# Operand sums of the feed-forward Strassen products moved from VectorE to ScalarE and accumulating DMAs, and three plain gate/up pairs a layer in place of four

## The chip, the cores and the metric

The kernel runs on one core of one Trainium2 chip. The time is the device time of one execution in microseconds (us), the median of several runs. The engines are TensorE (PE), VectorE (DVE), ScalarE (ACT), GpSimd (POOL) and SyncE (SP). Each engine takes its instructions in the order in which they stand in its own queue, and an instruction that waits holds up all that stand behind it.

## The reference

A two-layer decoder trunk on 512 positions of width 1024, all float32. Layer 0 mixes positions by dilated window attention, layer 1 by causal pooling; each is followed by a SwiGLU feed-forward part, with RMSNorm ahead of every part. The change is in the feed-forward part alone:

```
def rmsnorm(x, g):
    y = x * lax.rsqrt(jnp.mean(x * x, axis=-1, keepdims=True) + RMS_EPS)
    return y * g

def swiglu_ffn(h, w_gate_up, w_down):        # D_FF = 2816 = 22 blocks of 128
    gu = h @ w_gate_up
    gate, up = gu[..., :D_FF], gu[..., D_FF:]
    return (jax.nn.silu(gate) * up) @ w_down

x = x + swiglu_ffn(rmsnorm(x, ffn_norm[i]), w_ffn_gate_up[i], w_ffn_down[i])
```

## The kernel before

Positions lie along the free dimension (512 columns), channels along the 128 partitions: x is eight tiles X[0] to X[7] of 128x512. Every float32 operand of a large product is split into two parts, `hi` (a rounded copy, by ACT) and `lo` (the rest, by DVE; `split`, L93 and L94, or `split_neg`, L97 and L98, for the negated value), and every product is three matmuls: hi by hi, hi by lo, lo by hi.

The feed-forward part (`ffn`) makes 22 gate/up pairs j = 0 to 21 and then the down products. A **plain pair** is two products of 8 k-steps by 3 matmuls of 512 columns, 48 matmuls (`Product.add`, L314 to L317). A **Strassen pair** (`chained`, with `mult`, L446 to L448) cuts gate and up, the channels and the positions into halves and needs seven products of 4 k-steps by 3 matmuls of 256 columns, 84 matmuls. The first `NPLAIN` = 4 pairs of a layer are plain, since the operands of the Strassen pairs must first be made out of the normalised x. In layer 0 the first part of the layer is pairs 0 to 5, and its down products follow; in layer 1 the first part is pairs 0 and 1, and their down products (8 products of 2 k-steps, 48 matmuls of 512) stand behind the plain pairs (`PARTS`).

The plain pairs do not wait for the normalisation: `lead` holds two and five eighths of their products ahead of it, on x times its weight, and each result is multiplied by the row of 1/rms (`row`, made on ACT at L415) when it is read out (L1029, L1035).

The operands of the Strassen pairs are made by `prepare(k)` for half pair k = 0 to 3, that is, for channel blocks k and k + 4. `normed` writes both normalised blocks to a buffer `h` (two L563 on DVE, 128x512 each). Its four quarters of 256 columns are h[0,0], h[0,1] (first block, left and right positions) and h[1,0], h[1,1]. DVE then makes the four sums "1" = h[0,1] - h[0,0], "2" = "1" - h[1,1], "3" = h[1,1] - h[1,0] and "4" = "2" + h[1,0] (negated), at L567, L568 and L570, into a second buffer. All operands are split: "11" and "21" (the left quarters), the sums, and "22" (negated). Both buffers are `Temp`, taken from two loose slots (`slot`), and are given back at the end of `prepare`. Each plain pair calls `prepare(j)` once.

Weights come by DMAs on SP's queue into four `raw` buffers, are split into five `w` buffers, and a Strassen pair's sums of weights are made by an accumulating DMA on POOL's queue (L161) and two additions on DVE (L177, L178). `pump`, called behind each product, issues loads and splits when buffers are free. The order on each engine is set by a scheduler when the program is built; it may put instructions of later calls ahead of earlier ones where their data allow it.

Of the kernel before, what the change touches and what calls it, by code (L numbers as in the profile page):

```python
# [10 lines left out]
AF = mybir.ActivationFunctionType  # L11
OP = mybir.AluOpType
# [4 lines left out]
S = 512  # L17
# [19 lines left out]
NF = 4  # L37
H2 = S // 2
K2 = KC // 2
NPLAIN = 4  # L40
WARM = 6
NSOLO = 3
PARTS = {0: ((0, 6, False), (6, 14, True), (14, 22, True)), 1: ((0, 2, False), (2, 10, True), (10, 18, True), (18, 22, False))}
# [21 lines left out]
def trunk(ctx: ExitStack, tc: tile.TileContext, xT, xN, norms, w_first, w_qk, w_qkp, w_v0, w_v0p, w_v12, w_out, w_pair, w_down, w_dblock, w_pin, w_pgrp,  # L65
          consts, ident_in, invcnt_in, outT, outR):
    nc = tc.nc
# [24 lines left out]
    def split(hi, lo, v):  # L92
        nc.scalar.activation(hi, v, AF.Copy)  # L93
        nc.vector.tensor_tensor(lo, v, hi.bitcast(F32), op=OP.subtract)  # L94

    def split_neg(hi, lo, v):
        nc.scalar.activation(hi, v, AF.Copy, scale=-1.0)  # L97
        nc.vector.scalar_tensor_tensor(lo, v, -1.0, hi.bitcast(F32), op0=OP.mult, op1=OP.subtract)  # L98
# [251 lines left out]
    held = {}  # L350

    def give(key):
        del taken[held.pop(key)]
# [202 lines left out]
        def done(self):  # L556
            del taken[self.i]

    def normed(layer, k, row, h, t, chained=False):

        for i in range(2):
            c = k + i * K2
            nc.vector.scalar_tensor_tensor(h.t[:, i * S:(i + 1) * S], X[c], nrm[:, layer, c:c + 1], row,  # L563
                                           op0=OP.mult, op1=OP.mult)
        hq = h.t.rearrange("p (a b c) -> p a b c", a=2, b=2)
        tq = t.t.rearrange("p (a b c) -> p a b c", a=2, b=2)
        nc.vector.tensor_sub(tq[:, :, 0], hq[:, :, 1], hq[:, 0])  # L567
        nc.vector.tensor_sub(t.t[:, H2:S], t.t[:, :H2], h.t[:, 3 * H2:])  # L568
        if chained:
            nc.vector.scalar_tensor_tensor(t.t[:, 3 * H2:], t.t[:, H2:S], -1.0, h.t[:, S:3 * H2], op0=OP.mult, op1=OP.subtract)  # L570
        else:
            nc.vector.tensor_add(t.t[:, 3 * H2:], t.t[:, H2:S], h.t[:, S:3 * H2])
        return h, t

    def halves_of(hi, lo):
        return [tuple(v[:, a * H2:(a + 1) * H2] for v in (hi, lo)) for a in range(2)]
# [8 lines left out]
    with tc.tile_pool(name="opool", bufs=1) as opool:  # L585
        early = opool.tile([P, HEADS, S], F32R, tag="o", name="early")
        with tc.tile_pool(name="apool", bufs=1) as apool:
            const = apool.tile([P, 5 * P], F32, name="const")
            d0, d12, swap = const[:, :2 * G], (const[:, 2 * G:2 * G + P], const[:, 2 * G + P:3 * G]), const[:, 3 * G:3 * G + P]
            rows = {}  # L590
# [250 lines left out]
            H, T, o = {}, {}, []  # L841

            def prepare(k):

                h, t = normed(0, k, rows["row"], Held("raw"), Held("raw"))
# [88 lines left out]
            for c in range(2):  # L934
                p = product(0)
# [69 lines left out]
    with tc.tile_pool(name="fpool", bufs=2) as fpool:  # L1005
# [3 lines left out]
        def ftile(name, n=S):  # L1009
            return fpool.tile([P, PAD + S], F32, tag="f", name=name, bufs=6)[:, :n]  # L1010
# [8 lines left out]
        def ffn(layer, nxt, lead, row):  # L1019

            op = nxt - 1
# [4 lines left out]
            def plain_pair(j, up):  # L1026
                pg = gu()
                gt = ftile("gt")
                nc.vector.tensor_mul(gt, pg, row)  # L1029
                prepare(j)  # L1030
                pu = gu()
                if j == NPLAIN - 1:
                    for k in range(KC):
                        give((op, k))
                nc.vector.tensor_mul(up, pu, row)  # L1035
                nc.scalar.activation(gt, gt, AF.Silu)
                nc.vector.tensor_mul(up, up, gt)

            T = {}

            def prepare(k):


                h, t = normed(op, k, row, Temp(), Temp(), True)
                hq, b22 = h.t.rearrange("p (a b c) -> p a b c", a=2, b=2), h.t[:, 3 * H2:]
# [3 lines left out]
                for i, names in enumerate((("1", "2"), ("3", "4"))):  # L1049
                    held["t", k, 1 + i], b = slot("tt", apart=True)  # L1050
                    split(b[:, 0], b[:, 1], t.t[:, i * S:(i + 1) * S])
                    for a, name in enumerate(names):
                        T[name, k] = tuple(b[:, e, a * H2:(a + 1) * H2] for e in range(2))
# [3 lines left out]
                split_neg(*n, b22)  # L1057
                T["22", k] = n
                h.done()
                t.done()  # L1060

            B, U, late = {}, {}, deque()

# [27 lines left out]
            def operands_left(i, v):  # L1091
# [5 lines left out]
            def later(f, *a):  # L1097
                return lambda: f(*a)

            def waiting():  # L1100
                hooks = {}
# [54 lines left out]
            j = 0  # L1156
# [280 lines left out]
```

## Time and profile before

| | |
|---|---|
| median of 3 runs | 1197.54 us (1196.87 to 1197.91) |
| the profiled execution | 1197.8 us |
| its span | 1196.0 us |
| granted TensorE clock | 0.998 |
| TensorE busy | 1184.6 us (99%) |
| VectorE busy | 997.2 us (83%) |
| ScalarE busy | 680.7 us (57%) |
| GpSimd busy | 147.0 us (12%) |

The span is the stretch from the first to the last instruction; 1.8 us of the profiled execution lie around it. Matmuls overlap each other in the records, so what one costs is the distance from its start to the next one's start, not its own duration. The feed-forward part of layer 0 begins with the row of 1/rms on ACT at 485.91 us of the span, that of layer 1 at 873.45 us.

### The profile page before, as it was taken

Reading aid. Unit: us, or ns where it says so; the run is one execution under the profiler, and the core shown is the slowest. Engines: PE = TensorE matmul, PEld = TensorE weight load, DVE = VectorE, ACT = ScalarE, POOL = GpSimd, SP = SyncE. Lnnn points to the kernel's source line nnn. Section 1 sums busy time; section 2 is a strip of 40 time slices with the busy share of each in tenths; the row PEclk is TensorE's granted clock in tenths of the full one; section 3 lists DMA queues with packets and bytes.
Section 4 is the critical chain, followed back from the end, with each engine's and each line's share of the span. In section 5 each row is a group of like instructions: output and inputs, shape, how many; then the busy total and the mean of one; then the engine's idle time right before and its main releaser. Section 6 shows DMA issues by size and latency. Waiting matters only on the chain.

```text
span 1196.0 us, 24858 instructions
## 1 busy us (share of the span) xinstructions
PE 1184.6 (99%) x9936; PEld 1118.9 (94%) x9936; DVE 997.2 (83%) x1730; ACT 680.7 (57%) x1214; POOL 147.0 (12%) x137
## 2 busy tenths in 40 slices
PE   9999999999999999999999999999999999999997
PEld 7889999999999988898999999998789999999996
DVE  6978898889788856895899889998989998898875
ACT  6445564555456643562677567763455776676553
POOL 1111211111111000101111111100310111111100
PEclk9999999999999999999999999999999999999999
DMA  8346656665766533336677777753153777777732
GB/s 277 124 103 163 156 154 161 170 159 150 189 149 163 163 133 122 88 115 158 160 197 188 194 201 199 186 171 124 53 122 93 191 196 198 196 191 199 189 86 72
DMA packets 73365, 188.42 MB, mean 158 GB/s; under 512 B 7312, under 2 KB 9504, under 8 KB 73248
## 3 DMA queue, kind: packets, MB, share of 16 engines
q1 hardware_dynamic: 50400, 141.98, 36.1%
q0 software_dynamic: 22704, 44.58, 23.1%
q8 instruction: 78, 1.28, 0.4%
q14 instruction: 39, 0.32, 0.1%
q10 hardware_dynamic: 144, 0.26, 0.1%
HBM read 184.70 MB, written 2.10 MB: 156 GB/s over the span
## 4 chain that ended last, share of the span: by engine, by line
PE 87%; DVE 6%; issue 3%; ACT 1%; DMA 1%; POOL 0%; SPq 0%; POOLq 0%; DVEq 0%; ACTq 0%
PE ps L446 19%; PE ps L447 18%; PE ps L448 18%; PE ps L314 7%; PE ps L315 7%; PE ps L317 7%; PE ps L617 2%; PE ps L619 2%; PE ps L618 2%; DVE w L94 2%; PE ps L829 1%; PE ps L701 1%; DVE s L1225 1%; ACT w L93 1%; PE ps L721 1%
## 5 line engine op out<-in xcount | busy, mean ns | idle before, releaser
L93 ACT ACTIVATE w<-raw 128x1024 fp32r<-128x1024 f32 (+1 forms) x299 | 313.5, 1056 | 213.7 <-PE ps L448 69.1
L94 DVE TENSOR_TENSOR w<-raw,w 128x1024 fp32r<-128x1024 f32 (+1 forms) x299 | 361.5, 1214 | 58.9 <-ACT w L93 55.5
L446 PE MATMUL ps<-far,w 128*128 128x256 f32 x916 | 251.9, 275 | 0.1
L447 PE MATMUL ps<-far,w 128*128 128x256 f32 x916 | 251.8, 275 | 0.0
L448 PE MATMUL ps<-far,w 128*128 128x256 f32 x916 | 251.8, 275 | 0.0
L446 PE MATMUL ps<-near,w 128*128 128x256 f32 x632 | 178.4, 282 | 0.4 <-ACT first L528 0.4
L447 PE MATMUL ps<-near,w 128*128 128x256 f32 x632 | 174.8, 277 | 0.0
L448 PE MATMUL ps<-near,w 128*128 128x256 f32 x632 | 174.8, 277 | 0.0
L446 PEld LDWEIGHTS ps<-far,w 128*128 128x128 f32 x916 | 171.8, 188 | 0.6 <-ACT first L528 0.5
L447 PEld LDWEIGHTS ps<-far,w 128*128 128x128 f32 x916 | 171.9, 188 | 0.1
L448 PEld LDWEIGHTS ps<-far,w 128*128 128x128 f32 x916 | 171.9, 188 | 0.0
L446 PEld LDWEIGHTS ps<-near,w 128*128 128x128 f32 x632 | 118.9, 188 | 1.3 <-ACT first L528 0.9
L447 PEld LDWEIGHTS ps<-near,w 128*128 128x128 f32 x632 | 118.8, 188 | 0.0
L448 PEld LDWEIGHTS ps<-near,w 128*128 128x128 f32 x632 | 118.8, 188 | 0.0
L315 PE MATMUL ps<-near,w 128*128 128x512 f32 (+1 forms) x284 | 106.6, 375 | 0.6 <-DVE near L379 0.6
L314 PE MATMUL ps<-near,w 128*128 128x512 f32 (+1 forms) x284 | 106.9, 377 | 0.0
L317 PE MATMUL ps<-near,w 128*128 128x512 f32 (+1 forms) x284 | 106.1, 374 | 0.0
L161 POOL DMA_DIRECT2D raw<-w_pair x36 | 43.6, 1212 | 359.7 <-DMA raw<-w_pair 174.8
L315 PEld LDWEIGHTS ps<-near,w 128*128 128x128 f32 x284 | 53.4, 188 | 11.0 <-DVE near L379 1.8
L317 PEld LDWEIGHTS ps<-near,w 128*128 128x128 f32 x284 | 53.3, 188 | 9.5
L314 PEld LDWEIGHTS ps<-near,w 128*128 128x128 f32 x284 | 53.3, 188 | 9.4
L93 ACT ACTIVATE half<-rawhalf 128x512 fp32r<-128x512 f32 x81 | 51.0, 631 | 14.7 <-PE ps L448 12.5
(315 smaller groups left out, 2749.7 us busy)
## 6 DMA issues: line engine op xcount, KB each, us to landing
raw<-w_pair SPq DMA_DIRECT2D x80, 512.0 KB, 4.3
raw<-w_qkp SPq DMA_DIRECT2D x36, 512.0 KB, 4.1
raw<-w_pair POOLq DMA_DIRECT2D x36, 512.0 KB, 7.4
raw<-w_dblock SPq DMA_DIRECT2D x32, 512.0 KB, 4.5
raw<-w_v SPq DMA_DIRECT2D x18, 512.0 KB, 4.4
raw<-w_qkp POOLq DMA_DIRECT2D x18, 512.0 KB, 7.5
rawhalf<-w_pair SPq DMA_DIRECT2D x36, 256.0 KB, 5.1
raw<-w_dblock POOLq DMA_DIRECT2D x16, 512.0 KB, 7.3
```

Source lines behind the costliest of these rows:

```text
L93: nc.scalar.activation(hi, v, AF.Copy)
L94: nc.vector.tensor_tensor(lo, v, hi.bitcast(F32), op=OP.subtract)
L161: nc.gpsimd.dma_start(self.b.rearrange("p (a c) -> p a c", a=2), self.src[:, None, 3 * n:].to_broadcast([P, 2, n]), accum_op=OP.add)
L314: nc.tensor.matmul(self.p[:, cols], w[0][:, s], mh[:, cols], start=self.done == 0, stop=False)
L315: nc.tensor.matmul(self.p[:, cols], w[0][:, s], ml[:, cols], start=False, stop=False)
L317: nc.tensor.matmul(self.p[:, cols], w[1][:, s], mh[:, cols], start=False, stop=self.done == self.n)
L446: nc.tensor.matmul(dst, w.t[0][:, c], th, start=k == 0 and not on, stop=False, skip_group_check=on)
L447: nc.tensor.matmul(dst, w.t[0][:, c], tl, start=False, stop=False, skip_group_check=on)
L448: nc.tensor.matmul(dst, w.t[1][:, c], th, start=False, stop=k == n - 1, skip_group_check=on)
L617: nc.tensor.matmul(o, mh, wh, start=k == 0, stop=False)
L618: nc.tensor.matmul(o, mh, wl, start=False, stop=False)
L619: nc.tensor.matmul(o, ml, wh, start=False, stop=k == K2 - 1)
```

## The change

`NPLAIN` becomes 3. `prepare` and a new `settle` share the work of half pair k. In `prepare(k)`, DVE writes h as before, and ACT writes four negated quarters, of 256 columns each, into two tiles `one` and `two` of the ring `f` (6 buffers). Four accumulating DMAs on POOL's queue, from on-chip memory to on-chip memory, then add the other terms: `one` becomes "1" and "2", `two` becomes "4" negated and "3". The second and the fourth of them, in the code's order, read what the first wrote. `settle(k)`, called two products or more later, splits these sums. Two half pairs are prepared in the first plain pair's gate step, one in each of the next two steps. Only `h` is now a `Temp`. The attention part's own `prepare` keeps its sums on DVE.

```
-NPLAIN = 4
+NPLAIN = 3
...
+                h = Temp()
+                hq = normed(op, k, row, h)
+                one, two = ftile("t"), ftile("t")
+                nc.scalar.activation(one[:, :H2], hq[:, 0, 0], AF.Copy, scale=-1.0)
+                nc.scalar.activation(two[:, H2:], hq[:, 0, 1], AF.Copy, scale=-1.0)
+                nc.gpsimd.dma_start(one[:, :H2], hq[:, 0, 1], accum_op=OP.add)
+                nc.scalar.activation(one[:, H2:], hq[:, 1, 1], AF.Copy, scale=-1.0)
+                nc.scalar.activation(two[:, :H2], hq[:, 1, 1], AF.Copy, scale=-1.0)
+                nc.gpsimd.dma_start(one[:, H2:], one[:, :H2], accum_op=OP.add)
+                nc.gpsimd.dma_start(two.rearrange("p (a c) -> p a c", a=2), hq[:, 1], accum_op=OP.add)
+                nc.gpsimd.dma_start(two[:, :H2], one[:, :H2], accum_op=OP.add)
...
+            def settle(k):
+
+                one, two = sums.pop(k)
+                for i, names in enumerate((("1", "2"), ("4", "3"))):
+                    held["t", k, 1 + i], b = slot("tt", apart=True)
+                    for a, name in enumerate(names):
+                        T[name, k] = tuple(b[:, e, a * H2:(a + 1) * H2] for e in range(2))
+                    if i == 0:
+                        split(b[:, 0], b[:, 1], one)
+                split(*T["3", k], two[:, H2:])
+                split_neg(*T["4", k], two[:, :H2])
+
+            steps_of = {(0, 0): (later(prepare, 0), later(prepare, 1)), (1, 0): (later(settle, 0), later(prepare, 2)),
+                        (1, 1): (later(settle, 1), later(prepare, 3)), (2, 0): (later(settle, 2),), (2, 1): (later(settle, 3),)}
```

Here the first number of a step is the plain pair, the second 0 for its gate product and 1 for its up product. In the changed file the four copies stand at L1050, L1051, L1053 and L1054, the four DMAs at L1052 ("1"), L1055 ("2"), L1056 (both halves of `two`) and L1057 ("4"); L1026 and L1035 read out gate and up, L1171 adds the down products.

On DVE, where layer 0's first half pairs are prepared (`temp` is h and, before, the sums; `far` holds the operands; `near` the activations; DMASW are the completion counts of POOL's DMAs), there stood before:

```order
L563 SCALAR_TENSOR_TENSOR temp<-x,nrm,row 128x512 x2
L1035 TENSOR_TENSOR up<-ps,row 128x512
L567 TENSOR_TENSOR temp<-temp 128x2x256 [waits DVE_49]
L1037 TENSOR_TENSOR up<-up,gt 128x512 [waits DVE_49,Activation_49]
L568 TENSOR_TENSOR temp<-temp 128x256 [waits DVE_49]
L94 TENSOR_TENSOR far<-temp,far 128x512 [waits Activation_49]
```

Now there stands, in the same place:

```order
L563 SCALAR_TENSOR_TENSOR temp<-x,nrm,row 128x512 x2
L94 TENSOR_TENSOR w<-raw,w 128x1024 [waits Activation_49]
L94 TENSOR_TENSOR far<-temp,far 128x512 [waits DVE_49,Activation_49]
L98 SCALAR_TENSOR_TENSOR far<-temp,far 128x256 [waits Activation_49]
L563 SCALAR_TENSOR_TENSOR temp<-x,nrm,row 128x512 [waits DMASW1_49,DMASW0_49,DVE_49]
L563 SCALAR_TENSOR_TENSOR temp<-x,nrm,row 128x512
L94 TENSOR_TENSOR far<-t,far 128x256 [waits Activation_49]
L1035 TENSOR_TENSOR up<-ps,row 128x512
```

The sums are gone from DVE, and the L563 of the next half pair, which writes the same buffer, waits for two of the DMAs. On POOL's queue in the same place, two instructions of the norm (L402) were followed by nothing but weight DMAs; now there stands:

```order
L402 TENSOR_TENSOR rcol<-var,nhalf 128x2 x2
L1052 DMA t<-temp 128x256
L1056 DMA t<-temp 128x512
L1055 DMA t<-t 128x256
L1057 DMA t<-t 128x256
L161 DMA raw<-w_pair 128x2x512
L1052 DMA t<-temp 128x256
L1056 DMA t<-temp 128x512
```

The DMA of `two` has moved ahead of that of "2", and a weight DMA stands between the first and the second half pair's.

On ACT, still in layer 0, the third half pair had these rows before (`gt` is the gate, L97 makes "22"):

```order
L1036 ACTIVATE gt<-gt 128x512
L93 ACTIVATE far<-temp 128x512
L97 ACTIVATE far<-temp 128x256
L93 ACTIVATE far<-temp 128x512 x2
L93 ACTIVATE near<-up 128x512
```

Now its four copies stand behind the splits of half pair 1's sums, which wait for that half pair's DMAs:

```order
L1036 ACTIVATE gt<-gt 128x512 [waits DVE_49]
L93 ACTIVATE far<-t 128x512 [waits DMASW7_49,DMASW5_49]
L97 ACTIVATE far<-t 128x256 [waits DMASW0_49]
L1050 ACTIVATE t<-temp 128x256 [waits DVE_49,Activation_49]
L1051 ACTIVATE t<-temp 128x256 [waits Activation_49]
L1053 ACTIVATE t<-temp 128x256 [waits DVE_49]
L1054 ACTIVATE t<-temp 128x256
```

The second row splits "1" and "2", the third "4".

On PE, in layer 0's first Strassen pair, the products stood one behind the other (before; the first name is the accumulator, the last the weight buffer):

```order
L446 MATMUL ps_6217<-far_5849,w_6043 128x256
L447 MATMUL ps_6217<-far_5849,w_6043 128x256
L448 MATMUL ps_6217<-far_5849,w_6043 128x256
L446 MATMUL ps_6219<-far_5849,w_6150 128x256
L447 MATMUL ps_6219<-far_5849,w_6150 128x256
L448 MATMUL ps_6219<-far_5849,w_6150 128x256
```

Now the first pair's products (ps_6183 to ps_6185) and the first two of the next pair (ps_6307, ps_6308) are mixed; 59 matmuls behind the first one there stands:

```order
L446 MATMUL ps_6308<-far_5851,w_6134 128x256
L447 MATMUL ps_6308<-far_5851,w_6134 128x256
L448 MATMUL ps_6308<-far_5851,w_6134 128x256
L446 MATMUL ps_6185<-far_5851,w_5969 128x256
L446 MATMUL ps_6183<-far_5851,w_6067 128x256
L447 MATMUL ps_6183<-far_5851,w_6067 128x256
```

The fourth of these rows is the first that reads "1" of half pair 3, and the fifth reads "2".

On DVE in layer 1, the split of pair 1's activation, which the down products read, stood before between the two L563 of half pair 2:

```order
L1029 TENSOR_TENSOR gt<-ps,row 128x512
L563 SCALAR_TENSOR_TENSOR temp<-x,nrm,row 128x512
L94 TENSOR_TENSOR near<-up,near 128x512
L563 SCALAR_TENSOR_TENSOR temp<-x,nrm,row 128x512
L94 TENSOR_TENSOR w<-raw,w 128x1024
```

Now it stands behind those of half pair 3, which wait for half pair 2's DMAs:

```order
L563 SCALAR_TENSOR_TENSOR temp<-x,nrm,row 128x512 x2
L1035 TENSOR_TENSOR up<-ps,row 128x512
L94 TENSOR_TENSOR far<-t,far 128x256
L1037 TENSOR_TENSOR up<-up,gt 128x512
L94 TENSOR_TENSOR far<-t,far 128x512
L94 TENSOR_TENSOR far<-temp,far 128x512
L98 SCALAR_TENSOR_TENSOR far<-temp,far 128x256
L94 TENSOR_TENSOR near<-up,near 128x512
```

More of the change, by code (lines that the diff above doesn't have):

```diff
@@ L557, in done, with normed @@
             del taken[self.i]
-    def normed(layer, k, row, h, t, chained=False):
+    def normed(layer, k, row, h):
         for i in range(2):
@@ L564, in normed @@
                                            op0=OP.mult, op1=OP.mult)
[L565 to L573, printed above, removed]
+        return h.t.rearrange("p (a b c) -> p a b c", a=2, b=2)
     def halves_of(hi, lo):
@@ L843, in prepare @@
             def prepare(k):
-                h, t = normed(0, k, rows["row"], Held("raw"), Held("raw"))
+                h, t = Held("raw"), Held("raw")
+                hq = normed(0, k, rows["row"], h)
+                tq = t.t.rearrange("p (a b c) -> p a b c", a=2, b=2)
+                nc.vector.tensor_sub(tq[:, :, 0], hq[:, :, 1], hq[:, 0])
+                nc.vector.tensor_sub(tq[:, 0, 1], tq[:, 0, 0], hq[:, 1, 1])
+                nc.vector.tensor_add(tq[:, 1, 1], tq[:, 0, 1], hq[:, 1, 0])
                 for i in range(2):
@@ L1029, in plain_pair @@
                 nc.vector.tensor_mul(gt, pg, row)
-                prepare(j)
+                for f in steps_of.get((j, 0), ()):
+                    f()
                 pu = gu()
@@ L1034, in plain_pair @@
                         give((op, k))
+                for f in steps_of.get((j, 1), ()):
+                    f()
                 nc.vector.tensor_mul(up, pu, row)
@@ L1037, in plain_pair, with later @@
                 nc.vector.tensor_mul(up, up, gt)
-            T = {}
+            T, sums = {}, {}
+            def later(f, *a):
+                return lambda: f(*a)
             def prepare(k):
-                h, t = normed(op, k, row, Temp(), Temp(), True)
-                hq, b22 = h.t.rearrange("p (a b c) -> p a b c", a=2, b=2), h.t[:, 3 * H2:]
+                h = Temp()
[9 more added lines that the diff above has]
+                nc.gpsimd.dma_start(two[:, :H2], one[:, :H2], accum_op=OP.add)
                 held["t", k, 0], b = slot("tb", apart=True)
@@ L1048, in prepare @@
                 T["11", k], T["21", k] = (tuple(b[:, e, i * H2:(i + 1) * H2] for e in range(2)) for i in range(2))
[L1049 to L1053, printed above, removed]
                 if k % 2 == 0:
@@ L1056, in prepare @@
                 n = tuple(T["n"][:, e, k % 2 * H2:(k % 2 + 1) * H2] for e in range(2))
-                split_neg(*n, b22)
+                split_neg(*n, hq[:, 1, 1])
                 T["22", k] = n
                 h.done()
-                t.done()
+                sums[k] = one, two
+            def settle(k):
[10 more added lines that the diff above has]
+                        (1, 1): (later(settle, 1), later(prepare, 3)), (2, 0): (later(settle, 2),), (2, 1): (later(settle, 3),)}
             B, U, late = {}, {}, deque()
@@ L1095, in operands_left @@
                 split(*B["4", i], u[:, H2:])
-            def later(f, *a):
-                return lambda: f(*a)
             def waiting():
```

## Prediction

> **What bounds the kernel now.** First the page: its span, its busy times and the chain that ended last.
>
> ```profile
> span 1196.0 us, 24858 instructions
> PE 1184.6 (99%) x9936; PEld 1118.9 (94%) x9936; DVE 997.2 (83%) x1730; ACT 680.7 (57%) x1214; POOL 147.0 (12%) x137
> PE 87%; DVE 6%; issue 3%; ACT 1%; DMA 1%; POOL 0%; SPq 0%; POOLq 0%; DVEq 0%; ACTq 0%
> ```
>
> TensorE sets the end: it is busy for 99% of the span and makes 87% of the chain. So the time falls only by fewer matmuls, and it rises by whatever makes PE wait. Whether PE can wait is read from the stages that the change touches. Here are the windows of layer 0's plain pairs (three pairs' time, then the fourth's) and of layer 1's (columns: length, busy us of PE, PEld, DVE, ACT, POOL, then clock, DMA share, GB/s):
>
> ```profile
> 486.50:505.50 19.00, 19.00 (x86) 15.70 (x85) 18.96 (x32) 11.72 (x19) 1.26 (x1) 1.00 0.34 80
> 505.50:516.40 10.90, 10.90 (x50) 9.03 (x49) 10.90 (x19) 5.96 (x10) 0.00 (x0) 1.00 0.14 37
> 874.00:893.00 19.00, 19.00 (x86) 15.73 (x85) 18.92 (x31) 10.83 (x18) 2.46 (x2) 1.00 0.54 132
> ```
>
> In these stages DVE is as full as PE (18.96 of 19.00 us, 10.90 of 10.90). The fourth plain pair is cover: it gives DVE 10.9 us more to make the operands.
>
> **What the change takes off PE.** The timeline of PE at the start of the first Strassen pair in layer 0, and the same in layer 1:
>
> ```profile
> 510.92 0.39 PE L314 MATMUL ps<-near,w 128*128 128x512 f32 x1
> ...
> 516.14 0.39 PE L317 MATMUL ps<-near,w 128*128 128x512 f32 x1
> 516.36 0.28 PE L446 MATMUL ps<-far,w 128*128 128x256 f32 x1
> ...
> 517.65 0.28 PE L448 MATMUL ps<-far,w 128*128 128x256 f32 x1
> ...
> 518.67 0.28 PE L448 MATMUL ps<-far,w 128*128 128x256 f32 x1
> ...
> 914.06 0.28 PE L446 MATMUL ps<-far,w 128*128 128x256 f32 x1
> ```
>
> From 510.92 to 516.14 there are 23 steps: 0.227 us for a matmul of 512. From 517.65 to 518.67 there are 9: 0.1133 us for one of 256. A plain pair takes 48 x 0.227 = 10.9 us, a Strassen pair 84 x 0.1134 = 9.53. One pair a layer changes kind: 2 x 1.36 = **2.7 us less work on PE**, and no other source of gain, since PE has next to no idle time.
>
> **What the change moves and adds.** Rows of DVE and ACT at layer 0's first half pair, and the row of layer 1:
>
> ```profile
> 487.14 1.41 DVE L563 SCALAR_TENSOR_TENSOR temp<-x,nrm,row 128x512 f32<-128x512 f32 x2
> 488.47 0.69 DVE L1035 TENSOR_TENSOR up<-ps,row 128x512 f32<-128x512 f32 x1
> 489.07 0.68 DVE L567 TENSOR_TENSOR temp<-temp 128x512 f32<-128x512 f32 x1
> ...
> 490.27 0.42 DVE L568 TENSOR_TENSOR temp<-temp 128x256 f32<-128x256 f32 x1
> 490.61 0.69 DVE L94 TENSOR_TENSOR far<-temp,far 128x512 fp32r<-128x512 f32 x1
> ```
>
> ```profile
> 485.91 0.60 ACT L415 ACTIVATE row<-ps 128x512 f32<-128x512 f32 x1 [2.85 <-PE ps L409]
> 487.31 1.28 ACT L1036 ACT_TABLE_LOAD   x1 [0.81 <-DVE gt L1029]
> 488.60 0.63 ACT L1036 ACTIVATE gt<-gt 128x512 f32<-128x512 f32 x1
> 489.14 0.62 ACT L93 ACTIVATE far<-temp 128x512 fp32r<-128x512 f32 x1
> 489.66 1.05 ACT L93 ACTIVATE w<-raw 128x1024 fp32r<-128x1024 f32 x1
> 490.61 0.40 ACT L97 ACTIVATE far<-temp 128x256 fp32r<-128x256 f32 x1
> 490.92 0.62 ACT L93 ACTIVATE far<-temp 128x512 fp32r<-128x512 f32 x1
> 873.45 0.60 ACT L415 ACTIVATE row<-ps 128x512 f32<-128x512 f32 x1 [3.76 <-PE ps L409]
> ```
>
> By start to start, a 512 row costs DVE 0.60 us, a 256 row 0.34, the two L563 together 1.33; ACT takes 0.31 for a 256 row, 0.55 for 512, 0.95 for a weight split. DVE loses 0.60 + 2 x 0.34 = 1.28 us a half pair, 10.2 us in all. ACT gains four copies, 1.25 us a half pair, and POOL four DMAs. None of this is on the path by its length. What is on the path is a chain of waits, which DVE's sums, each right behind the last, did not have: a copy, a DMA, a second DMA that needs the first, a split.
>
> **What one DMA costs.** The trace has no accumulating DMA within the chip. The rows near to it (columns of the issue rows: count, size, us from issue to landing; first the one weight DMA of POOL that ran with the DMA engines otherwise idle):
>
> ```profile
> raw<-w_pair POOLq DMA_DIRECT2D x1, 512.0 KB, 6.5
> ```
>
> ```profile
> raw<-w_pair SPq DMA_DIRECT2D x80, 512.0 KB, 4.3
> raw<-w_down SPq DMA_DIRECT2D x8, 128.0 KB, 2.3
> out<-x SPq DMA_DIRECT2D x8, 128.0 KB, 1.8
> out<-ends SPq DMA_DIRECT2D x3, 256.0 KB, 2.3
> invcnt<-invcnt_in POOLq DMA_DIRECT2D x1, 8.0 KB, 3.2
> q0 software_dynamic: 22704, 44.58, 23.1%
> ```
>
> ```profile
> L161 POOL DMA_DIRECT2D raw<-w_pair x36 | 43.6, 1212 | 359.7 <-DMA raw<-w_pair 174.8 <-ACT w L93 50.2 <-DVE u L537 34.0
> L961 POOL DMA_DIRECT2D x<-xN x8 | 4.3, 552 | 32.3 <-PE ps L618 32.3
> ```
>
> POOL's queue moved 44.58 MB in 23.1% of 1196 us: 161 GB/s while it moved, 3.25 us for 512 KB. Of the 6.5 us that leaves 6.5 - 1.21 (issue) - 3.25 = 2.0 fixed. A source on the chip saves about 0.5 (1.8 against 2.3 us for 128 KB on SP). With 0.55 for the issue, as in L961, and 0.8 or 1.6 for the bytes: **a = 2.9 us for a DMA of 256 columns (128 KB), b = 3.7 for L1056 (256 KB)**. From below: SP's rows plus 0.2 for the longer issue, a = 2.0, b = 2.5. From above: the straight line between POOL's 8 KB (3.2) and 512 KB (6.5), a = 4.0, b = 4.8. I take the first, since L161 is nearest in kind: POOL issues it, and it accumulates.
>
> **Layer 0, in us from the row at 485.91.** Before the first copy ACT has the table load, the Silu and a weight split, to 4.4; the fourth copy ends at 5.7, so half pair 0's L1056 issues at 5.8. Then:
>
> - All half pairs get the same `temp` slot, since h is now the only one taken. So half pair 1's L563 waits on DVE until L1056 has landed, 5.8 + b. Two L563 and four copies later (2.7) its L1056 issues: 8.5 + b.
> - Its L1057 writes the same bytes and waits for that landing: 8.5 + 2b, and lands at 8.5 + a + 2b. On ACT the split of "4" stands ahead of half pair 2's copies: 0.4 + 1.3 later, half pair 2's L1056 issues at 10.2 + a + 2b.
> - Half pair 3's h starts at 10.2 + a + 3b. Its L1052 issues 1.2 later, L1055 a later, that lands another a later, and the split takes 0.65: "1" of half pair 3 is there at 12.05 + 3a + 3b = **31.9**.
>
> PE starts the Strassen pair at 516.36 - 485.91 - 10.9 = 19.55 and has 59 matmuls ahead of the first that needs it: to 26.3. It waits 5.6 us, and about 1.3 more for operands split behind it on ACT and DVE (three rows of 0.4, an estimate): **6.9**. The weight DMA on POOL between half pairs 0 and 1 I cost at nothing: half pair 1's L1056 issues at 12.2 by the chain, and the weight DMA is issued by 11.2 (DVE frees its buffer at 5.7, SP's load lands 4.3 later, the issue takes 1.2).
>
> **Layer 1, from 873.45.** No table load: half pair 0's L1056 issues at 4.5. Half pair 1's h starts at 4.5 + b, L1052 follows 1.2 later, L1055 lands at 5.7 + 2a + b. ACT then has the split of "1" and "2", the Silu, a weight split and four copies, 3.4: half pair 2's L1056 issues at 9.1 + 2a + b. Half pair 3's L563 wait for it on DVE until 9.1 + 2a + 2b. Behind these, and behind four copies and three splits on ACT, stands the split of pair 1's activation, 4.1 later: 13.2 + 2a + 2b = 26.4. Here the down products are 10.9 us of cover ahead of the Strassen pair, but they need that activation. PE comes to them at 914.06 - 873.45 - 2 x 10.9 = 18.8 and has 18 matmuls that don't: to 22.9. It waits **3.5**.
>
> The sum: 6.9 + 3.5 - 2.7 = 7.7 us more than the profiled execution's 1197.8, of which 1196.0 are the span. The runs' median is 1197.5, so I forecast **1205.3**.
>
> **Rivals.**
>
> - *Short DMAs (not slower).* Place: the same chains. With a = 2.0, b = 2.5, layer 0's "1" is there at 25.6, before PE wants it; layer 1's activation at 22.2. Left are the smaller waits, which are DVE's own rows: rows of 23.8 us stand ahead of the split of "1" (ten of 0.60 for gates and ups, 5.3 for h, 8.5 of operand splits, 3.4 of weight splits, 0.6), behind a start at 0.7 and 1.9 of wait for ACT, 26.4. So 1.4 to 2.0 in layer 0 and none in layer 1, less 2.7: -0.7 to -1.3, 1196.2 to 1196.8. The sum above is 5(a + b) - 25.3, so the waits outweigh the gain from a + b = 5.1 on. For it: 1.8 us in SP's row; against it: 3.2 us for POOL's smallest transfer. [...]
> - *Slow DMAs.* The upper ends: 38.5 - 26.3 + 1.3 = 13.5 in layer 0, 30.8 - 22.9 = 7.9 in layer 1, less 2.7: +18.7, 1216. For it: a small DMA may move its bytes behind a 512 KB weight DMA on the same queue (half pair 1's does in layer 0).
> - *The full gain.* DVE's 5.1 us a layer less is enough, no wait reaches PE: 1194.8. DVE was full for 29.9 us, and only 19 are left: against it.
> - *It doesn't do what it says:* PE starts the Strassen pair late for want of its weights, though operands are there. In the chain of before ACT and DMA have 1% each, so weights come in time now, and I give it little.
>
> **Chances.** Forecast (1201 to 1211) 0.47; short DMAs (1196 to 1200) 0.27; slow ones (1211 to 1218) 0.2; full gain 0.03; late weights, 1200 to 1206, 0.03. The range 1196.2 to 1216.0 takes in both ends. 0.2%, 2.4 us, is about what a measurement of this kernel can tell from no change: faster 0.04, same 0.26, slower 0.70.
>
> **What would show it.** Right: PE gaps ahead of L446 to L448 just behind the third plain pair in layer 0, ended by ACT's split of `t`, and ahead of L314 of the down products in layer 1; L563 of `temp` with a wait for DMA, some 7 us apart; L1052 and L1055 landing in about 2.9 us, L1056 in 3.7. Wrong: landings near 2 us, DVE without gaps there, and PE's gaps ended by DVE's rows alone.

## The result, and the profile after

The changed kernel takes **1225.99 us** (median of 5 runs, 1225.16 to 1227.66) against 1197.54: a ratio of 1.0243, 95% interval 1.0231 to 1.0254, 28.4 us slower. The forecast was 1205.3, its range 1196.2 to 1216.0. The sign was right, the size was not.

The page of the changed kernel, span, busy times and chain:

```profile
span 1223.4 us, 25151 instructions
PE 1189.9 (97%) x10008; PEld 1124.8 (92%) x10008; DVE 995.0 (81%) x1726; ACT 694.2 (57%) x1266; POOL 177.6 (15%) x171
PE 84%; issue 5%; DVE 4%; DMA 4%; ACT 2%; POOL 2%; POOLq 0%; DVEq 0%; SPq 0%; ACTq 0%
```

The span grew by 27.4 us. PE has fallen from 99% to 97%, and DMA went from 1% to 4% of the chain. Who PE waited for, in total, times and longest:

```profile
PE ps L446 <- ACT far L93: 11.3, 3, 8.7
PE ps L314 <- DVE up L1035: 8.7, 1, 8.7
PE ps L314 <- ACT near L93: 2.5, 1, 2.5
```

These are the predicted places: ahead of layer 0's first Strassen pair, and ahead of layer 1's first down products. PE's rows at the first of them, its windows around it (columns as in the prediction), and layer 1's:

```profile
505.39 0.28 PE L448 MATMUL ps<-far,w 128*128 128x256 f32 x1
514.39 0.58 PE L446 MATMUL ps<-far,w 128*128 128x256 f32 x1 [8.72 <-ACT far L93]
515.50 0.41 PE L448 MATMUL ps<-far,w 128*128 128x256 f32 x1
515.71 0.41 PE L446 MATMUL ps<-far,w 128*128 128x256 f32 x1
...
518.40 0.28 PE L447 MATMUL ps<-far,w 128*128 128x256 f32 x1
```

```profile
505.00:510.00 5.00, 0.67 (x6) 0.47 (x5) 0.72 (x2) 0.74 (x2) 1.34 (x2) 0.80 0.81 196
510.00:515.00 5.00, 0.58 (x1) 0.29 (x1) 3.82 (x8) 4.48 (x11) 2.08 (x3) 0.50 0.36 53
515.00:520.00 5.00, 4.32 (x22) 4.12 (x23) 3.33 (x8) 2.55 (x7) 2.53 (x4) 0.67 0.76 118
```

```profile
917.94 0.79 PE L314 MATMUL ps<-near,w 128*128 128x512 f32 x1 [8.70 <-DVE up L1035]
922.05 2.93 PE L314 MATMUL ps<-near,w 128*128 128x512 f32 x6 [2.47 <-ACT near L93]
```

PE did only six matmuls of the Strassen pair and stopped for 8.7 us. Then it went on at half speed: from 515.50 to 515.71 is 0.21 us for a matmul of 256 columns that took 0.1133 before, until 518.3. The granted clock falls to 0.50 in these windows. DVE, full here before (5.00 of 5.00 us in each window), is busy for 0.72 and 3.82 us in the first two.

The whole loss can be added up from PE's rows, over 45 us from each layer's row of 1/rms on: the time from each matmul's start to the next one's, less 0.227 or 0.1134. The steps that are more than 0.3 us too long make 12.4 us in layer 0 and 12.5 in layer 1; the shorter ones make 2.6 and 3.1, of which 4.2 in all are steps at the lower clock. That is 30.6 us. The kernel before has 0.4 of it too, and 2.7 is gained: **27.5, where the span grew by 27.4.** Below, "stage waits" are the sums of the long steps. (Forecasts below that give 13.1 and 5.7 for layer 1 count some of the half-speed matmuls as waits.)

What DVE and POOL did in layer 0, and how long the DMAs of two stretches took to land (in the last column):

```profile
497.70 1.41 DVE L563 SCALAR_TENSOR_TENSOR temp<-x,nrm,row 128x512 f32<-128x512 f32 x2 [5.09 <-DMA t<-temp]
509.28 1.42 DVE L563 SCALAR_TENSOR_TENSOR temp<-x,nrm,row 128x512 f32<-128x512 f32 x2 [4.42 <-DMA t<-temp]
517.67 0.75 DVE L563 SCALAR_TENSOR_TENSOR temp<-x,nrm,row 128x512 f32<-128x512 f32 x1 [1.67 <-DMA t<-temp]
```

```profile
490.50 0.95 POOL L1052 DMA_DIRECT2D t<-temp  x1 [6.03 <-ACT t L1051]
491.39 0.96 POOL L1056 DMA_DIRECT2D t<-temp  x1
496.41 0.89 POOL L1055 DMA_DIRECT2D t<-t  x1 [4.07 <-DMA t<-temp]
...
498.62 1.43 POOL L161 DMA_DIRECT2D raw<-w_pair  x1
499.63 1.36 POOL L1052 DMA_DIRECT2D t<-temp  x1
500.73 1.15 POOL L1056 DMA_DIRECT2D t<-temp  x1
508.24 0.86 POOL L1055 DMA_DIRECT2D t<-t  x1 [6.37 <-DMA t<-temp]
```

From 490 to 491.9:

```profile
raw<-w_pair SPq DMA_DIRECT2D x1, 512.0 KB, 4.5
t<-temp POOLq DMA_DIRECT2D x1, 256.0 KB, 6.2
t<-temp POOLq DMA_DIRECT2D x1, 128.0 KB, 5.4
```

From 499.5 to 501.5:

```profile
raw<-w_pair POOLq DMA_DIRECT2D x1, 512.0 KB, 7.3
raw<-w_pair SPq DMA_DIRECT2D x1, 512.0 KB, 7.4
t<-temp POOLq DMA_DIRECT2D x1, 256.0 KB, 8.4
t<-temp POOLq DMA_DIRECT2D x1, 128.0 KB, 8.3
```

Half pair 0's DMAs run beside one weight load of SP and land in 5.4 and 6.2 us. Half pair 1's are issued right behind POOL's weight DMA, L161, beside a load of SP: 8.3 and 8.4. Half pair 3's last ones, with nothing beside them, take 2.6 and 3.3. In layer 1 it is half pair 0 that comes behind a weight DMA: L161 is issued at 889.63, and L1052 and L1056, at 890.40 and 891.10, land in 8.2 and 8.9 us. On DVE, L1035 of the first pair stands behind the first of these waits and starts at 499.36; before, it started at 488.47. DVE's own rows are not what holds these DMAs: the L1057 issued at 517.90 landed in 2.6 us with DVE busy all the while, and the four that took 8.2 to 8.9 us had DVE busy for 17 to 63% of the time.

### The profile page after: what moved, and what is told of

It is laid out like the page before. It is cut to its first block, busy times and chain, and to the rows that moved or that the text cites. A ratio compares the mean times of both kernels' runs of the same rounds, so it can differ in the third digit from the quotient of the medians.

```text
span 1223.4 us, 25151 instructions
## 1 busy us (share of the span) xinstructions
PE 1189.9 (97%) x10008; PEld 1124.8 (92%) x10008; DVE 995.0 (81%) x1726; ACT 694.2 (57%) x1266; POOL 177.6 (15%) x171
## 4 chain that ended last, share of the span: by engine, by line
PE 84%; issue 5%; DVE 4%; DMA 4%; ACT 2%; POOL 2%; POOLq 0%; DVEq 0%; SPq 0%; ACTq 0%
PE ps L446 19%; PE ps L448 19%; PE ps L447 19%; PE ps L314 5%; PE ps L315 5%; PE ps L317 5%; DMA t<-temp 2%; PE ps L609 2%; PE ps L611 2%; PE ps L610 2%; PE ps L821 1%; DVE w L94 1%; PE ps L693 1%; DMA raw<-w_pair 1%; DMA t<-t 1%
## 5 line engine op out<-in xcount | busy, mean ns | idle before, releaser
L446 PE MATMUL ps<-far,w 128*128 128x256 f32 x964 | 266.5, 277 | 11.5 <-ACT far L93 11.3
L447 PE MATMUL ps<-far,w 128*128 128x256 f32 x964 | 265.6, 276 | 0.1
L448 PE MATMUL ps<-far,w 128*128 128x256 f32 x964 | 265.3, 276 | 0.0
L446 PEld LDWEIGHTS ps<-far,w 128*128 128x128 f32 x964 | 181.6, 189 | 13.1 <-ACT far L93 11.9
L447 PEld LDWEIGHTS ps<-far,w 128*128 128x128 f32 x964 | 181.5, 188 | 0.6 <-DVE far L94 0.4
L448 PEld LDWEIGHTS ps<-far,w 128*128 128x128 f32 x964 | 181.5, 188 | 0.0
L446 PEld LDWEIGHTS ps<-near,w 128*128 128x128 f32 x632 | 118.9, 188 | 1.3 <-ACT first L528 0.9
L448 PEld LDWEIGHTS ps<-near,w 128*128 128x128 f32 x632 | 118.8, 188 | 0.0
L447 PEld LDWEIGHTS ps<-near,w 128*128 128x128 f32 x632 | 118.8, 188 | 0.0
L314 PE MATMUL ps<-near,w 128*128 128x512 f32 (+1 forms) x252 | 95.4, 383 | 11.2 <-DVE up L1035 8.7
L161 POOL DMA_DIRECT2D raw<-w_pair x38 | 46.4, 1221 | 362.1 <-DMA raw<-w_pair 144.0
L315 PE MATMUL ps<-near,w 128*128 128x512 f32 (+1 forms) x252 | 95.4, 379 | 0.8 <-DVE near L379 0.6
L317 PE MATMUL ps<-near,w 128*128 128x512 f32 (+1 forms) x252 | 94.7, 377 | 0.0
L314 PEld LDWEIGHTS ps<-near,w 128*128 128x128 f32 x252 | 48.1, 191 | 20.6 <-DVE up L1035 9.1
L177 DVE TENSOR_TENSOR raw<-raw 128x512 f32<-128x512 f32 x83 | 56.8, 684 | 2.6 <-issue 1.3
L315 PEld LDWEIGHTS ps<-near,w 128*128 128x128 f32 x252 | 48.2, 191 | 10.5 <-DVE near L379 1.8
```

The costliest lines, as they stand in the source:

```text
L161: nc.gpsimd.dma_start(self.b.rearrange("p (a c) -> p a c", a=2), self.src[:, None, 3 * n:].to_broadcast([P, 2, n]), accum_op=OP.add)
L177: nc.vector.tensor_add(a[:, :n], a[:, :n], b[:, :n])
L314: nc.tensor.matmul(self.p[:, cols], w[0][:, s], mh[:, cols], start=self.done == 0, stop=False)
L315: nc.tensor.matmul(self.p[:, cols], w[0][:, s], ml[:, cols], start=False, stop=False)
L317: nc.tensor.matmul(self.p[:, cols], w[1][:, s], mh[:, cols], start=False, stop=self.done == self.n)
L446: nc.tensor.matmul(dst, w.t[0][:, c], th, start=k == 0 and not on, stop=False, skip_group_check=on)
```

## The experiments

The theory: the accumulating DMAs are short, but late where a weight load moves its bytes at the same time; DVE (next h, same buffer) and ACT (next split) stand behind each landing; PE stops, and its clock drops behind a long stop (to 0.50 behind 8.7 us). Rivals: the chain of waits is long however fast the DMAs; three plain pairs are too few on any route; another engine's extra work.

**1. POOL's weight DMAs left out** of three pairs.

```
-            nc.gpsimd.dma_start(self.b ...)
+            if not self.skip:       # (layer, pair) (0, 5), (1, 4), (1, 5)
+                nc.gpsimd.dma_start(self.b ...)
```

> The kernel after, but three of POOL's weight DMAs (L161, 512 KB each) are left out: that of layer 0's pair 5, which the trace shows between half pairs 0 and 1, and those of layer 1's pairs 4 and 5. These pairs compute with weights that lack one addition. Theory Q (queue): the small DMAs issued behind such a weight DMA move their bytes only after its bytes, so they land in 7 to 9 us where they else take 2.7 to 3.4. Then L1052 and L1056 of half pair 1 land in at most 5 us, PE's 8.7 us wait in layer 0 falls to below 4 us, that of layer 1 by 3 us or more, the low clock behind both goes, and the time is 1204 to 1216. Rival L (length): the waits are the DMAs' own fixed times, one behind the other; the weight DMA hardly matters, and the time is 1221 to 1226.

Measured: 1218.76 us, ratio 1.0173 (1.0158 to 1.0189): 7 us less than the change, but outside both forecasts. Stage waits 10.2 and 7.7 us. DMAs issued from 500 to 502 in layer 0:

```profile
raw<-w_pair SPq DMA_DIRECT2D x1, 512.0 KB, 5.9
t<-temp POOLq DMA_DIRECT2D x1, 256.0 KB, 6.3
t<-temp POOLq DMA_DIRECT2D x1, 128.0 KB, 2.7
```

L1052, ahead of SP's load (501.89), takes 2.7 us in place of 8.3; L1056, which that load overlaps, still 6.3. So POOL's weight DMAs are one part, and SP's loads another.

**2. The same three transfers on SP's queue**, not accumulating.

```
+            if self.skip:
+                nc.sync.dma_start(self.b ..., self.src ...)
```

> The same three weight DMAs, with the same bytes from the same place into the same tile, but issued on SP's queue and without accumulating (these pairs compute with other weights). Theory Q (queue): what counts is that the small DMAs stand in the same queue behind it, so this is like the run without these DMAs: 1204 to 1216, small DMAs at most 5 us. Rival S (shared engines): what counts is the bytes that the 16 DMA engines have to move in that time, from whichever queue; then half pair 1's DMAs still take 7 us or more, and the time is 1219 to 1228.

Measured: 1225.81 us, 1.0235 (1.0214 to 1.0256). The time is theory S's, but not for its reason: SP issued the transfer at 495.60, 3 us earlier than POOL had, and it landed at 500.35, just as half pair 1's DMAs were issued (500.23). The first of these landed in 2.7 us and the second, beside SP's next load, in 5.8. The stage waits are 10.3 and 11.8 us. So the run's time does not tell a shared queue from shared engines.

**3 and 4. The sums on DVE, and on GpSimd,** with three pairs, one h and the two stages.

```
-                (four copies, four DMAs)
+                nc.vector.tensor_sub(one[:, :H2], hq[:, 0, 1], hq[:, 0, 0])
+                nc.vector.tensor_sub(one[:, H2:], one[:, :H2], hq[:, 1, 1])
+                nc.vector.tensor_sub(two[:, H2:], hq[:, 1, 1], hq[:, 0, 1])
+                nc.vector.tensor_add(two[:, :H2], one[:, H2:], hq[:, 1, 0])
```

> The kernel after with three plain pairs, one h buffer and the two stages, but each half pair's four copies and four DMAs replaced by four sums of 256 columns on DVE (0.34 us each, 5.4 us a layer). If the loss is in the route of the sums (copies, DMAs, their landings), L563 never waits for a DMA and PE waits in layer 0 for DVE's rows alone, 3 to 5 us, in layer 1 below 3, with some low clock behind: 1198 to 1206. Rival N (number of pairs): three plain pairs are too little time whatever route the sums take, and the time is above 1212.

Measured: **1202.48 us**, 1.0039 (1.0024 to 1.0054). The same three pairs, 23.5 us faster than with DMAs and 4.9 slower than the kernel before: the number of pairs is a small part of the loss at most. PE's waits in layer 1, the longest of this run's stages:

```profile
PE ps L314 <- ACT near L93: 1.4, 1, 1.4
PE ps L314 <- DVE up L1035: 1.2, 1, 1.2
```

The stops are short, and the granted clock is 1.00 in every window of layer 0's stage. In layer 1 it is not. Both stops fall within 3.6 us there (897.66 to 901.24), PE is busy for only 1.03 of 3.40 us, and the clock then falls to 0.50 for 3.4 us:

```profile
897.60:901.00 3.40, 1.03 (x4) 0.48 (x3) 3.40 (x6) 0.97 (x3) 0.00 (x0) 1.00 0.00 0
901.00:904.50 3.50, 3.27 (x8) 2.59 (x9) 3.50 (x8) 0.81 (x2) 0.00 (x0) 0.51 0.02 5
```

With `nc.gpsimd` in place of `nc.vector`:

> As the run with the sums on DVE, but the four sums of a half pair are GpSimd instructions (the trace has 1.54 us for a 512-column product there, L369; so 0.8 us each, 3.1 us a half pair, 12.4 us a layer). If the loss is in the landings of the DMAs, h is free 3.2 us behind its second L563, against 6 to 11 us in the kernel after, and PE waits some 0 to 4 us a layer: 1196 to 1205. If any wait of DVE on another engine at this place costs as much, 1212 or more. A third way: GpSimd's sums slow DVE's rows beside them, seen as longer rows of DVE in the window, and the time is 1205 to 1212.

Measured: 1213.91 us, 1.0134 (1.0119 to 1.0149): in size the second forecast, by its rows the third and the second together, since DVE's h waits for the sums too and the stage waits are 6.0 and 9.1 us. GpSimd's sums and DVE's splits beside them, in layer 0 (mean ns behind the total):

```profile
L1050 POOL TENSOR_TENSOR t<-temp 128x256 f32<-128x256 f32 x4 | 8.0, 2000 | 7.7 <-DVE temp L563 7.7
L1053 POOL TENSOR_TENSOR t<-t,temp 128x256 f32<-128x256 f32 x4 | 4.3, 1072 | 0.0
```

```profile
L94 DVE TENSOR_TENSOR far<-temp,far 128x512 fp32r<-128x512 f32 x4 | 3.8, 951 | 0.0
```

A sum takes 1.0 to 2.0 us, not 0.8, and a split on DVE 951 ns in place of 684. Still 12 us faster than the DMAs.

**5. The loads held** until the accumulating DMAs of the layer have landed.

```
+            if self.late is not None:    # pairs (0, 5), (1, 4), (1, 5)
+                for t in (self.a, self.b, self.c):
+                    nc.gpsimd.tensor_copy(t[:, :1], marks[self.late])
```

(`marks[layer]` is one column copied from half pair 3's `two`.)

> The kernel after, but the weight loads of layer 0's pair 5 and of layer 1's pairs 4 and 5 (SP's transfers and POOL's) start only when half pair 3's last DMA of that layer has landed: a one-column copy by GpSimd from its result into each raw tile stands ahead of them. Nothing of the work is left out. So the accumulating DMAs have the DMA engines to themselves. Theory S (shared engines): they all land in 2.6 to 3.4 us; with a = 2.7 and b = 3.3 in the prediction's own sum, 5(a + b) - 25.3 = +4.7, so 1202, and with some us for late weights of the held pairs and for low clock behind waits of over 3 us, 1201 to 1209. Rival L (length): the landings hardly change the end, since DVE and ACT queue behind any landing; then above 1215.

Measured: 1244.92 us, 1.0394 (1.0378 to 1.0409). The time lies in rival L's range, but for another reason: the held weights came too late for their pairs. The stages ahead of that, 36 us from the row of 1/rms, answer the question. All the DMAs, over the run, and PE's waits in layer 0:

```profile
t<-temp POOLq DMA_DIRECT2D x8, 256.0 KB, 3.3
t<-t POOLq DMA_DIRECT2D x16, 128.0 KB, 2.7
t<-temp POOLq DMA_DIRECT2D x8, 128.0 KB, 2.7
```

```profile
507.29 0.39 PE L453 MATMUL ps<-far,w 128*128 128x256 f32 x1 [0.97 <-ACT far L93]
...
512.67 0.38 PE L453 MATMUL ps<-far,w 128*128 128x256 f32 x1 [1.88 <-ACT far L93]
518.72 0.65 PE L453 MATMUL ps<-far,w 128*128 128x256 f32 x2 [2.09 <-ACT far L93]
...
534.71 0.58 PE L453 MATMUL ps<-far,w 128*128 128x256 f32 x1 [4.16 <-ACT sums L531]
```

With the DMA engines to themselves they land in 2.6 to 3.7 us (one in 4.1), and the stage waits are 6.1 us in layer 0 (12.4 in the changed kernel) and 5.5 in layer 1 (12.5). About half of the waits are the weight loads' doing. It is not that DVE had fewer weight splits to make: its weight work in these 36 us is 5.6 and 6.2 us, against 4.3 in either layer of the changed kernel. The row at 534.71 is the new loss: the held weights.

**6. Two buffers for h.**

```
+                if prev:
+                    prev.pop().done()
+                prev.append(h)
```

> The kernel after, with the weight loads as they are, but h alternates between the two loose slots, so the h of half pair k + 1 no longer waits for the DMAs of half pair k that read h. If DVE's wait for that one slot carries the slow landings to PE, PE's 8.7 us waits fall to below 4 us each and the time is 1203 to 1214. If ACT's splits of the sums, which stand ahead of the next copies in ACT's order and wait for the same DMAs, carry them as much, little changes: 1219 to 1226.

Measured: 1216.63 us, 1.0159 (1.0144 to 1.0174), between the two. DVE's wait for that buffer, 11.2 us in layer 0 of the changed kernel, is gone; the stage waits are 8.4 and 10.0, since ACT still stands behind the landings:

```profile
ACT far L93 <- DMA t<-temp: 6.7, 4, 3.4
```

**7. Four plain pairs** with the new preparation (`NPLAIN = 4`).

> The kernel after, with its copies, DMAs, one h and two stages, but four plain pairs a layer as before (10.9 us more of cover, and 1.36 us more of matmuls, a layer). If the loss is waits that the fourth pair covered, PE waits in all below 3 us and the time is 1197 to 1201. If DVE's and ACT's waits for DMAs in the midst of the plain pairs stop PE there as well (gate and up results are read late and no bank of PSUM is free), 1205 or more.

Measured: 1226.98 us, 1.0245 (1.0229 to 1.0260): as slow as with three, the second forecast. The fourth pair hides next to nothing: it brings 2.7 us more of matmuls, and the time is 1.0 us longer. Over 75 us from the row of 1/rms, the long steps make 10.4 and 12.5 us. POOL and ACT in layer 0:

```profile
489.59 1.26 POOL L161 DMA_DIRECT2D raw<-w_pair  x1 [4.97 <-DMA raw<-w_pair]
490.36 1.42 POOL L1052 DMA_DIRECT2D t<-temp  x1
491.28 1.39 POOL L1056 DMA_DIRECT2D t<-temp  x1
```

```profile
500.74 0.42 ACT L93 ACTIVATE far<-t 128x256 fp32r<-128x256 f32 x1 [8.99 <-DMA t<-temp]
...
527.28 2.00 ACT L93 ACTIVATE w<-raw 128x1024 fp32r<-128x1024 f32 x2 [0.63 <-DVE raw L178]
...
530.65 0.35 ACT L520 COPY first<-ps 128x256 f32<-128x256 f32 x1
```

Here the weight DMA is issued ahead of half pair 0's, which land in 9.3 and 9.4 us. ACT stands idle for 9.0 us, DVE for 8.3. That time is missed later: the Strassen pair's own read-out (L520) is behind weight splits that ACT and DVE had not come to, and PE waits 4.6 us for it. So, as these rows read, what a landing costs is not only the end of its own chain: two engines that were full lose the time, and it comes back on PE as a backlog.

**8. PE kept busy** with 30 idle matmuls at both places.

```
+            for i in range(30):
+                nc.tensor.matmul(p[:, :P], ident, ident, start=True, stop=True)
```

> The kernel after, with 30 matmuls of 128 columns more at each of the two places where PE waits for 8.7 us (ahead of layer 0's first Strassen pair and of layer 1's first down product); they work on a constant tile, and the next product overwrites their result. Theory C (clock): of the 30.1 us lost, 22.5 are waits and some 5 to 8 are matmuls at half clock behind them (0.58 to 0.64 us in the rows instead of 0.28 and 0.39); PE kept busy, the granted clock stays at 1.00 there and the time falls to 1217 to 1222 though PE has more to do. Rival W (waits alone): the slow matmuls are no loss of their own, since what they work on comes no earlier; the time stays within 1224 to 1230.

Measured: 1234.36 us, 1.0311 (1.0293 to 1.0328): outside both. PE is busy at clock 1.00 to 512.3, then waits 2.1 and 5.3 us for the same operands as before, and the clock drops then:

```profile
505.00:510.00 5.00, 5.00 (x48) 5.00 (x47) 0.68 (x2) 0.70 (x2) 1.30 (x2) 1.00 0.79 192
...
515.00:520.00 5.00, 0.50 (x2) 0.30 (x2) 3.34 (x8) 2.56 (x6) 2.54 (x4) 0.66 0.76 119
```

The order of the matmuls behind the idle ones changed as well, so the run doesn't price the clock. In it the clock reads 1.00 to 516, 0.66 from 516 to 518 and 0.50 from 518 to 526, so it falls only behind PE's stops; the 4.2 us of the changed kernel are read from rows, not tested.

**9. The loads left out**; the weight splits are kept, on a column of zeros.

```
+            if self.skip:        # pairs (0, 5), (1, 4), (1, 5), (1, 6)
+                return
```

> The kernel after, but the weight loads that run during the plain pairs are left out, SP's and POOL's: those of layer 0's pair 5 and of layer 1's pairs 4, 5 and 6; these pairs compute with weights of zero, and all splits and sums of weights are still made. It is the run with the loads held, without its late weights. Theory S (small DMAs land late because weight loads move their bytes in the same time): all accumulating DMAs land in 2.6 to 3.4 us, PE waits in the two stages as in that run (4.9 and 3.9 us, and 2 to 3 in small waits), little low clock; with 2.7 us gained, 1203 to 1210. The prediction's own sum with a = 2.7, b = 3.3 gives 1202.5. Rival L (each landing, however short, costs the same waits on DVE and ACT): above 1214.

Measured: 1217.76 us, 1.0167 (1.0152 to 1.0183), above the theory and in rival L's range. In layer 0 the theory's condition is not met: the buffers left free let the next loads come earlier, into the same stage, L1056 landed in up to 6.0 us, and the stage waits are 9.3. The row of 1/rms itself comes 3.2 us later than in the changed kernel (488.48). In layer 1, where the stage stayed free of loads, the stage waits are 4.9, near the 5.5 with the loads held, and all weight splits are still made. From layer 1's row of 1/rms to the end this run takes 327.3 us, the changed kernel 337.0, the kernel before 322.6.

**10 and 11. Half of the sums on DVE**, h in two buffers; "3" and "4" by two DMAs a half pair, then by GpSimd.

```
+                nc.vector.tensor_sub(one[:, :H2], hq[:, 0, 1], hq[:, 0, 0])
+                nc.vector.tensor_sub(one[:, H2:], one[:, :H2], hq[:, 1, 1])
```

> Three plain pairs; sums 1 and 2 of a half pair, which PE needs first, on DVE (0.68 us a half pair, 2.7 a layer), sums 3 and 4 by ACT's copies and two accumulating DMAs (L1056 and L1057 of the kernel after), split one to two half pairs later; h alternates between two slots; loads as they are. If DMA landings cost time only where something is queued behind them, this has no DVE wait for a DMA, and DVE 2.7 us a layer less to do than with all sums on it (1202.5): 1197 to 1201. If landings of 5 to 9 us still stop ACT ahead of its next splits, it is slower than that run: 1203 to 1210.

Measured: 1215.66 us, 1.0154 (1.0139 to 1.0169): slower than all on DVE by 13 us, more than either forecast. The DMAs land in up to 8.8 us, and ACT waits for them (3.7, 1.3, 0.7, 1.0, 3.6 and 1.1 us in layer 0).

> As the run with sums 1 and 2 on DVE, but sums 3 and 4 are two GpSimd instructions (about 1 us each, as measured with all four there). If GpSimd's sums cost only what they hold up, 1198 to 1202. If they slow DVE's rows beside them (0.95 us in place of 0.68 for a split of 512 columns was seen with all four), DVE loses half of that run's loss: 1203 to 1208.

Measured: 1210.58 us, 1.0108 (1.0091 to 1.0125). A sum on GpSimd takes 1.5 to 1.8 us, and DVE's splits beside it 816 ns; slower than both forecasts. Neither beats the kernel before, and no version tried here does.

**12. Loads held and two buffers for h**, runs 5 and 6 together.

> The run with the loads held, and h alternating between two slots as well. Its time holds the late weights of the held pairs (that run: 1244.9), so what is read is PE's wait in the two stages of plain pairs and first Strassen pair: 6.1 us in layer 0 and 5.7 in layer 1 with the loads held and one h, 12.4 and 13.1 in the kernel after. If the one h slot makes what is left (DVE's h waits for a landing), below 3 us a stage. If ACT's splits of the sums, which wait for two landings in a row and stand ahead of the next copies, make it, 4 to 6 us a stage as before. The time, with late weights as in that run, 1236 to 1245.

Measured: 1243.19 us, 1.0381 (1.0363 to 1.0398). Stage waits 4.1 and 4.9 us, from 6.1 and 5.5. So of the waits that are left when the DMAs run alone, the one h slot makes some 2 us in layer 0 and 0.6 in layer 1; the rest is there with either buffer, and ACT's waits for landings are what its rows still show (up to 2.1 us).

## Why the prediction was wrong

The forecast was 6.9 + 3.5 - 2.7 = +7.7. Measured, on the same lines: 12.4 + 12.5 - 2.7, and 5.3 of short steps beyond those of the kernel before, most of it the clock: +27.5.

- **Right: the gain.** PE's rows account for the span with 2.7 us less work and no other gain.
- **Right: the price of a DMA alone.** a was taken as 2.9 us and b as 3.7; they are 2.7 and 3.3 (run 5). The issue takes 0.86 us at least, not 0.55, which is inside these numbers.
- **Right in kind, and lucky in size: the chain.** In layer 0 "1" of half pair 3 was forecast for 31.9 us behind the row of 1/rms. With the loads held PE gets it at 518.72 - 485.89 = 32.8. In the changed kernel that is 525.69 - 485.27 = 40.4. But with the measured a = 2.7 and b = 3.3 the same chain gives 30.1, and the sum gives 7.4 us of waits where run 5 has 6.1 + 5.5. The prices were a little too high and the chain too short, and the two errors nearly cancel.
- **The step that failed** is "The weight DMA on POOL between half pairs 0 and 1 I cost at nothing: half pair 1's L1056 issues at 12.2 by the chain, and the weight DMA is issued by 11.2." Its issue was indeed out of the way; its bytes were not. The step looked at when POOL is free and not at when the DMA engines are, and it left SP's loads out altogether. h of half pair 1 starts 12.4 us behind the row of 1/rms, where 5.8 + b = 9.5 was worked out, and h of half pair 3 32.4, where 24.2 was. Two landings of 6.2 and 8.4 us in place of 3.7 make 7.2 of these 8.2 us. The sum for layer 1 has no weight DMA at all, though half pair 0's DMAs stood behind one there. The slow-DMA rival named the place in layer 0, and even it took b for 4.8 at most. In the two stages, weight loads cost 24.9 - 11.5 = **13.4 us of waits**.
- **A second step was too kind.** "59 matmuls ahead of the first that needs it": PE stopped behind six, since half pair 2's own quarters were late too, with h. Counting cover for the last operand alone misses that every half pair's operands hang on the chain. With the loads held PE stops behind six as well, for 1.0 us. This and the rest that the chain leaves out are worth some 4 us: 11.5 with the DMAs alone, where the sum with the measured prices gives 7.4.
- **A term was missing:** PE's clock behind its stops, 4.2 us of short steps. In the changed kernel the stops of 8.7 us led to a granted clock of 0.50 and, in layer 0, to half-speed rows from 514.39 to 518.3. In layer 1 of the run with the sums on DVE two stops of 1.2 and 1.4 us led to it too, with PE busy for 1.03 of 3.40 us, so a long stop is not needed. The "waits of over 3 us" in the expectation of run 5 are no limit that the runs show: in run 7 the rows behind two stops of 2.6 and 0.3 us (517.06 to 520.36, layer 0) are at half speed as well, 0.21 us a matmul of 256 columns.
- The *short-DMA* rival, 0.27, was wrong too: it needed a + b below 5.1, and alone the DMAs take 6.0. "DVE's 5.1 us a layer less is enough" never counted: DVE stood idle 11.2 us for the buffer of h in layer 0.

What stays open is how a load delays a small DMA: because the engines are shared, or also because POOL's queue is. The first case needs no queue, since POOL's had nothing ahead of L1052. From 492.5 to 496.5 the DMA engines were 100% busy at 219 GB/s, and the 896 KB under way there (one load, L1052 and L1056) take 4.2 us at that rate, so bytes alone can explain it. How the engines share their time between queues that have work at once, no run here shows.

Some cases bear on the queue. In layer 1 of the changed kernel an L1055 (128 KB) issued at 922.40, 0.7 us behind an L161, took 7.0 us to land, as L161 did, and SP's next load came only at 927.73. Run 6 has such a case at 498.53 (7.4 us), run 8 one at 928.43 (7.1 us). In layer 1 of run 2, 128 KB issued at 889.13, 0.7 us behind a load of SP's and with nothing ahead in POOL's queue, took 4.7 us, and that load took 4.8. Each of these small DMAs landed 0.6 to 0.7 us behind the load issued ahead of it, whichever queue that stood in. So they show no cost of the queue beyond the length of the load, but no run set out to test it.

## What to carry to other kernels

Here a DMA's duration went with the bytes in flight while it ran (128 KB: 2.7 us alone, 5.4 beside one weight load, 8.3 behind one and beside another): before moving an on-chip sum to a DMA, list the loads of that stage, on every queue, not just the issues ahead of it. A DMA in place of an instruction on a full engine saved nothing here, since work behind it on that engine, and on another that was needed, waited for its landing; the time saved was lost as idle time and came back as a backlog (run 7: ACT idle for 9.0 us, later PE for 4.6), which one more pair of cover did not hide. And stops of TensorE cost more than their length here: matmuls at half speed for 3.9 us behind one of 8.7 us, and for 3.4 us behind two of 1.2 and 1.4 us close together.

## What the runs showed of the hardware

- An accumulating DMA within the chip took 2.6 to 3.3 us for 128 KB (median 2.7, one 4.1) and 3.2 to 3.7 for 256 KB (median 3.3) with no weight load beside it (run 5), of which POOL's issue is 0.86 at least; 5.4 (128 KB) and 6.2 (256 KB) beside one 512 KB load of SP's (changed kernel, layer 0); 8.2 to 8.9 behind a 512 KB accumulating DMA of the same queue with another load beside it (changed kernel, both layers; 9.3 and 9.4 in run 7), and 7.0 to 7.4 (128 KB) behind one with no other load until shortly before its landing (changed kernel, runs 6 and 8).
- The granted clock fell to 0.50 some 2.4 to 5 us after the start of PE's 8.7 us stops (changed kernel), and matmuls ran at half speed for 3.9 us after the first of them. It fell behind two stops of 1.2 and 1.4 us within 3.6 us as well (sums on DVE, layer 1), and matmuls ran at half speed behind two of 2.6 and 0.3 us (run 7, layer 0); it stayed at 1.00 behind single stops of 1.9 and 2.1 us (loads held, layer 0).
- GpSimd's additions of 256 columns took 1.0 to 2.0 us and DVE's 512-column splits beside them 816 to 951 ns (runs 4 and 11), where 684 is usual.
